# Window attention of the decode samples: from VectorE multiply-adds behind the state loop to matmuls ahead of it

## The chip, the cores and the metric

One Trainium2 chip, all 8 cores, each with an eighth of the work: 2048 tokens of a prompt and 16 of the 128 decode samples. The metric is the device time of the slowest core, in microseconds. Some executions fall in a slower state, in which the cores of one die or of both run at a lower granted clock; the comparisons below use fast runs alone.

A second measure is needed, because most of what is at stake lies in one short stretch. I call it the **sample stretch**: from the first matmul of the samples' input projection to the first activation of the last feed-forward's norm. It is read from the timeline of each of the eight cores of the profiled execution, and I quote the median of the eight, or the slowest core's value where I say so. In the kernel before it is 397.1 us in the median and 403.0 on the slowest core.

## The reference, cut to what matters

A layer is a half-step feed-forward, a mixer and a second half-step feed-forward. The mixer has four mLSTM heads and eight heads of window attention (SWA) with two shared key/value heads. For a decode sample the attention looks at 128 cached keys and values and at its own new one, with a sink:

```python
k_all = concatenate([buf_k, k]); v_all = concatenate([buf_v, v])
s = einsum('bqkgd,bskd->bkgqs', qg, k_all) * dh ** -0.5
mx = maximum(max(s), sink); p = exp(s - mx)
p = p / (sum(p) + exp(sink - mx))
o = einsum('bkgqs,bskd->bqkgd', p, v_all)
```

with 16 samples per core, 128 + 1 positions, two key/value heads of 64 and four query heads to each. The mLSTM of a sample updates a state of four 128x128 matrices (`c_new = decay * c + w * v k^T`) and reads it with q.

## The kernel before

Each core runs two passes over its tokens (feed-forward, then a pipelined mixer), then `sample_mixer` for its 16 samples, then the last feed-forward. A small scheduler derives the waits from keys: each operation names what it reads and writes, and a wait is made for the last writer, and before a write for the readers. Two names that share a key wait for one another, whether the bytes overlap or not. The parts of `sample_mixer` that matter:

```python
# mLSTM state loop: 4 groups of 4 samples
for bt in range(4):
    dma('sp', Cst, sC0_d[...], ['bigs'], ['bigs', 'Cst'], 'cst')        # 1 MB of state
    dma('sp', qrow, scr_d[0, ...].to_broadcast(...), ['scr0', 'bigs'], ['qrow'], 'qrow')  # 1 MB
    dma('sp', krow, scr_d[1, ...].to_broadcast(...), ['scr1', 'bigs'], ['krow'], 'krow')  # 1 MB
    prod = Cst * qrow; Cq = reduce(prod)                                # VectorE
    for j in range(16): Cst[j] *= decay[j]; Cst[j] += krow[j] * wv[j]   # VectorE
    dma('sp', sC_d[...], Cst, ['Cst'], [], 'cout')
# ... outputs of the mLSTM half into yTs[:, 0:4]; norms of q and k ...
# attention: one (sample, head) per partition, 128 of them
for g_, kv, p0, hd in PO:          # 8 x 4 small transfers: q, new k, new v, sink
    dma('sp', qx[p0:p0 + NS, :], qns[:, hd * 64:(hd + 1) * 64], ...)
    # [cut: kxn, vxn, sinkx alike]
load_kv(cK_d)                      # 8 transfers: each key head loaded for its 4 query heads
for d_ in range(64): Sx += Kx[:, :, d_] * qx[:, d_]        # VectorE, 128x128 each
load_kv(cV_d)                      # into the same buffer Kx
# [cut: softmax]
for d_ in range(64): ox[:, d_] = sum(Px * Kx[:, :, d_])    # VectorE
# [cut: 8 transfers back, cast, 4 transposes into yTs[:, 4:8]]
# output projection of the samples: 16 matmuls of yTs with w_out
```

`qrow` and `krow` name the key `bigs`, which the load of `Cst` writes, so they wait until it has landed.

Names used below: `rep` holds the gate factors of the 16 samples, sent through DRAM so that all 128 partitions get them; `wv` is v times one of these factors, the product that first needs `rep`; the first product of a group is `Cst * qrow`, 128x2048; `gon` is the gain of the mLSTM's output norm. In the changed kernel I call the part of the attention ahead of the state loop, from the norms to the scores, the **prelude**; `snew` is the score of a sample's own new key, `Vnd` its new value and `Vdup` the V cache, both written twice in bf16. SP is the queue from which nearly all these transfers are issued, in order.

## Time and profile before

| kernel before | |
|---|---|
| time, median of 4 runs | 3423.82 us (3419.25 to 3429.88) |
| sample stretch, slowest core | 403.0 us |
| of it the attention (norms to transposed result) | 218.8 us |
| VectorE's waits for the K and V caches in it | 76.5 + 56.9 us |
| three gaps between the groups of the state loop | 53.0 us of VectorE idle |
| last feed-forward, matmul part | 480 us at clock 0.99 |

Read it in this order: the slices show where TensorE is empty, the table of windows prices the hole, the timeline shows its order, the chain shows what waits for what. The lines stand in the prediction.

### The profile page before, as it was taken

How to read it: one execution, taken by the hardware profiler on the slowest of the kernel's cores; microseconds unless marked ns; L12 is line 12 of the kernel's file. 1: busy time of each engine (PE TensorE's matmuls, PEld its weight loads, DVE VectorE, ACT ScalarE, POOL GpSimd, SP SyncE). 2: the span in 40 equal slices, each digit the busy share in tenths (PEclk: the TensorE clock that was granted, in tenths of full speed). 3: DMA queues.
4: the chain of work that ended last, by engine and by line, in shares of the span. 5: the costliest groups of instructions: out<-in, count | busy, mean ns of one | idle time of the engine just before them, and what ended most of it. 6: DMA issues, size and time to landing. Idle time of an engine off the chain costs nothing.

```text
span 3423.5 us, 37344 instructions; the slowest of 8 cores (3394.0 to 3423.5 us)
## 1 busy us (share of the span) xinstructions
PE 2189.6 (64%) x12789; PEld 1145.4 (33%) x12789; DVE 1124.3 (33%) x2719; ACT 752.6 (22%) x1760; POOL 108.3 (3%) x151
## 2 busy tenths in 40 slices
PE   0499999565189999755655555555300001699999
PEld 0244444343144444333433333333100001344444
DVE  1223233454212222334434344343343222122223
ACT  1310100332420101133333433333100003311100
POOL 0000000000000100000000000000000000000000
PEclk9999999776599999977766777667655555799999
DMA  6032330503220402240000000000032892122222
GB/s 147 1 50 32 43 42 2 78 1 95 48 38 13 62 13 44 36 66 1 1 1 1 1 1 1 1 1 2 18 124 75 61 49 44 19 32 44 32 44 99
DMA packets 152241, 124.93 MB, mean 36 GB/s; under 512 B 42956, under 2 KB 132340, under 8 KB 151000
## 3 DMA queue, kind: packets, MB, share of 16 engines
q0 software_dynamic: 93744, 65.58, 14.0%
q1 hardware_dynamic: 58312, 56.98, 8.7%
q8 instruction: 105, 1.72, 0.2%
q14 instruction: 80, 0.66, 0.1%
HBM read 174.82 MB, written 15.24 MB: 56 GB/s over the span
## 4 chain that ended last, share of the span: by engine, by line
PE 56%; DVE 16%; ACT 9%; issue 8%; DMA 7%; SPq 4%; DVEq 1%; ACTq 0%; POOL 0%; POOLq 0%
PE ps L215 52%; SPq L212 4%; PE ps L218 3%; ACT sb_hT L228 3%; ACT sb_hn L228 2%; DVE sb_hn L257 2%; DMA sb_big<-win 2%; ACT sb_tmpC L228 2%; DMA sb_gain<-n 1%; DVE sb_CT L812 1%; DVE sb_hT L767 1%; ACT sb_sg L228 1%; DMA sb_big<-sC 1%; DVEq L124 1%; DVE sb_mixb L1105 1%
## 5 line engine op out<-in xcount | busy, mean ns | idle before, releaser
L215 PE MATMUL ps<-sb_hT,sb_wgu 128*128 128x512 bf16 (+1 forms) x4928 | 937.8, 351 | 1.2 <-ACT sb_hT L228 1.2
L215 PEld LDWEIGHTS ps<-sb_hT,sb_wgu 128*128 128x128 bf16 x4928 | 433.1, 98 | 506.5 <-issue 12.2
L215 PE MATMUL ps<-sb_big 128*128 128x512 bf16 (+1 forms) x2200 | 476.9, 379 | 0.0
L306 DVE TENSOR_TENSOR sb_big<-sb_sg,ps 128x512 bf16<-128x512 f32 x308 | 185.4, 613 | 756.7 <-PE ps L215 753.5
L228 ACT ACTIVATE sb_sg<-ps 128x512 f32<-128x512 f32 x308 | 165.8, 538 | 1101.8 <-PE ps L215 1101.7
L215 PEld LDWEIGHTS ps<-sb_big 128*128 128x128 bf16 (+1 forms) x2200 | 213.6, 97 | 259.9 <-issue 2.5
L322 DVE SCALAR_TENSOR_TENSOR sb_x<-ps,sb_x 128x512 f32<-128x512 f32 x288 | 199.2, 692 | 258.1 <-PE ps L215 258.1
L215 PE MATMUL ps<-sb_big,sb_hT 128*128 128x512 bf16 (+3 forms) x944 | 270.1, 448 | 8.5 <-DMA sb_big<-win 7.4
L218 PE MATMUL ps<-sb_identb,sb_hn 128*128 128x128 bf16 (+1 forms) x528 | 66.1, 303 | 298.6 <-DVE sb_hn L257 297.9
L228 ACT ACTIVATE sb_hT<-ps 128x1024 bf16<-128x1024 bf16 (+5 forms) x201 | 159.3, 792 | 397.3 <-PE ps L218 321.6
L218 PE MATMUL ps<-sb_identb,sb_hT 128*128 128x128 bf16 (+1 forms) x345 | 38.8, 261 | 323.3 <-DVE sb_hT L767 84.0
L218 PEld LDWEIGHTS ps<-sb_identb,sb_hn 128*128 128x128 bf16 (+1 forms) x528 | 51.5, 138 | 310.4 <-issue 310.4
L215 PEld LDWEIGHTS ps<-sb_big,sb_hT 128*128 128x128 bf16 (+1 forms) x944 | 104.0, 116 | 139.3 <-issue 94.1
L257 DVE SCALAR_TENSOR_TENSOR sb_hn<-sb_x,sb_stat,sb_gain 128x1024 bf16<-128x1024 f32 x48 | 61.7, 1285 | 249.8 <-ACT sb_stat L228 189.5
L218 PEld LDWEIGHTS ps<-sb_identb,sb_hT 128*128 128x128 bf16 (+1 forms) x345 | 26.5, 115 | 345.5 <-issue 345.5
L218 PE MATMUL ps<-sb_identb,sb_mixb 16*128 16x16 bf16 x4 | 0.3, 170 | 219.7 <-DVE sb_mixb L1127 219.7
L215 PE MATMUL ps<-sb_hT,sb_big 128*128 128x128 bf16 (+2 forms) x1600 | 115.3, 236 | 16.2 <-DMA sb_big<-win 16.2
L215 PEld LDWEIGHTS ps<-sb_hT,sb_big 128*128 128x128 bf16 (+1 forms) x1600 | 104.3, 102 | 28.7 <-issue 25.2
L212 POOL DMA_DIRECT2D sb_wgu<-wg x33 | 29.8, 903 | 2516.0 <-DVE sb_tmpA L1144 1648.4
L215 PE MATMUL ps<-sb_wgu,sb_hn 128*128 128x512 bf16 x256 | 92.5, 541 | 20.3 <-ACT sb_hn L228 20.3
L215 PE MATMUL ps<-sb_mixb,sb_onesf 128*128 128x64 f32 x2 | 0.7, 433 | 164.0 <-DVE sb_mixb L1066 164.0
L215 PE MATMUL ps<-sb_hT,sb_selT 4*128 4x1 f32 (+1 forms) x384 | 77.2, 305 | 0.0
(224 smaller groups left out, 1695.1 us busy)
## 6 DMA issues: line engine op xcount, KB each, us to landing
sb_wgu<-wg POOLq DMA_DIRECT2D x33, 512.0 KB, 7.8
sb_wgu<-wu POOLq DMA_DIRECT2D x33, 512.0 KB, 9.4
sb_big<-wd POOLq DMA_DIRECT2D x66, 256.0 KB, 9.8
sb_big<-win POOLq DMA_DIRECT2D x10, 1024.0 KB, 28.2
sb_x<-xa SPq DMA_DIRECT2D x16, 512.0 KB, 22.9
sb_x<-xb SPq DMA_DIRECT2D x16, 512.0 KB, 12.3
sb_big<-scr SPq DMA_DIRECT2D x8, 1024.0 KB, 6.9
yb<-sb_x SPq DMA_DIRECT2D x16, 512.0 KB, 2.6
```

Source lines behind the costliest of these rows:

```text
L124: eng.wait_ge(sems[key], v)
L212: P.add(q, lambda e: e.dma_start(out=out, in_=in_), r=r, w=w, dma=key)
L215: P.add('pe', lambda e: e.matmul(out, lhsT, rhs, start=start, stop=stop), r=r, w=w)
L218: P.add('pe', lambda e: e.transpose(out, in_, ident), r=r, w=w)
L228: P.add('act', lambda e: e.activation(out, in_, func, **kw), r=r, w=w)
L257: dve(lambda e: e.scalar_tensor_tensor(hs, xap, rs, gain[0:nt, :], ALU.mult, ALU.mult), [xkey, sk_, 'gain'], ['hn%d' % slot])
L306: dve(lambda e, ao=ao, sgs=sgs, ups=ups: e.tensor_tensor(ao, sgs, ups, ALU.mult), ['sg%d' % s2, 'b%d' % (2 + s2)], ['act%d.%d' % (jl, ti)])
L322: dve(lambda e, xh=xh, pb=pb: e.scalar_tensor_tensor(xh, pb, 0.5, xh, ALU.mult, ALU.add), ['b%d' % bk, xkey], [xkey])
L767: dve(lambda e, h=h, qo=qo: e.scalar_tensor_tensor(qnS[:, qo:qo + 64], qaps[:, h * 64:(h + 1) * 64], rq[:, h:h + 1], gqb, ALU.mult, ALU.mu ...
L812: dve(lambda e, h=h: e.scalar_tensor_tensor(CTv[:, h, :], CTv[:, h, :], decay_[:, h:h + 1], psb[4][:, h * 128:(h + 1) * 128], ALU.mult, AL ...
L1105: dve(lambda e, d_=d_: e.scalar_tensor_tensor(Sx, Kx[:, :, d_], qx[:, d_:d_ + 1], Sx, ALU.mult, ALU.add), ['Kx'] + M, M)
```

## The change

The intent: do the scores and the weighted sum on TensorE, load each cache once, start both loads early, and place the attention so that its latencies lie in other waits. The core of the diff (cuts marked):

```diff
-        dma('sp', n0s, sn0_d, [], WINKEYS + ACTKEYS + ['bigs'], 'sio')
+        dma('sp', n0s, sn0_d, [], WINKEYS + ACTKEYS + ['bigs', 'Cst', 'qrow', 'krow', 'prod'], 'sio')
+        dma('sp', K_all, cK_d.rearrange("b s f -> s b f"), [], HK + ['Kall'], 'kall')
+        dma('sp', V_all, cV_d.rearrange("b s f -> s b f"), [], HK + ['Vall'], 'vall')
 ...     # gates; rep goes through DRAM to be broadcast; wv = R(1) * vT
+        # norms of q and k (moved here), qpm = cast of q, 4 transposes -> qsT
+        # snew = q.k_new, by a product, a reduce and a small matmul
+        for quad in range(4):                      # 16 fp32 transposes of K, ScalarE evicts
+            ... tr(psb[bk][...], K_all[:, quad * 4 + j, :], identf) ...
+        Vdup = V_all twice, in bf16                # 2 VectorE copies of 128x2048
+        for kv in range(2):
+            for b in range(NS): mm(psb[4 + kv][:, b * 4:b * 4 + 4], KT[pr, b, :], qsT[pr, :, b], ...)
+        # STs, one transpose -> S_ps: one (sample, head) per partition again
         for bt in range(4):
-            dma('sp', Cst, ..., ['bigs'], ['bigs', 'Cst'], 'cst')
-            dma('sp', qrow, ..., ['scr0', 'bigs'], ['qrow'], 'qrow')
-            dma('sp', krow, ..., ['scr1', 'bigs'], ['krow'], 'krow')
+            dma('sp', Cst, ..., [], ['Cst'], 'cst')
+            dma('sp', qrow, ..., ['scr0'], ['qrow'], 'qrow')
+            dma('sp', krow, ..., ['scr1'], ['krow'], 'krow')
+            if bt == 0: # 16 sink transfers, 4 cache outputs
 ...         # the group's work and its store, unchanged
+            if bt == 0: # softmax on S_ps, transposes of P, 2 + 32 matmuls with Vnd and Vdup,
+                        # eviction straight into yTs[:, 4:8]
-        # the whole VectorE attention, its 40 small transfers and 16 cache loads
```

More of the change, by code (lines that the diff above doesn't have):

```diff
@@ L167, in build_nc @@
     swam_d = din("swam", [128, 256]); swam0_d = din("swam0", [128, 256]); amask_d = din("amask", [128, 2])
-    sel_d = din("sel", [4, 512])
+    sel_d = din("sel", [4, 512]); esel_d = din("esel", [128, 16])
     yb_d = dout("yb", [TOK, D]); ys_d = dout("ys", [NS, D])
@@ L192, in build_nc @@
     maskbig = sb("maskbig", [128, 128]); swam = sb("swam_t", [128, 256]); swam0 = sb("swam0_t", [128, 256])
-    amask = sb("amask_t", [128, 2]); selT = sb("selT", [68, 512])
+    amask = sb("amask_t", [128, 2]); selT = sb("selT", [4, 512]); esel = sb("esel_t", [128, 16])
     epsb = sb("epsb", [128, 1]); onesb = sb("onesb", [128, 128], BF16); onesf = sb("onesf", [128, 128])
@@ L242, in build_nc @@
     dma('sp', amask[:, :], amask_d, [], ['amask'], 'c0')
+    dma('sp', esel[:, :], esel_d, [], ['esel'], 'c0')
     dve(lambda e: e.memset(selT[:, :], 0.0), [], ['selT'])
@@ L997, in sample_mixer @@
         dma('sp', m0t, sm0_d, ['tmpA'], ['tmpA'], 'G_sin')
-        dma('sp', n0s, sn0_d, [], WINKEYS + ACTKEYS + ['bigs'], 'sio')
+        dma('sp', n0s, sn0_d, [], WINKEYS + ACTKEYS + ['bigs', 'Cst', 'qrow', 'krow', 'prod'], 'sio')
+        R_ = hT[:, :]
+        K_all = R_[:, 0:4096].bitcast(F32).rearrange("p (b f) -> p b f", f=128)
+        V_all = R_[:, 4096:8192].bitcast(F32).rearrange("p (b f) -> p b f", f=128)
+        dma('sp', K_all, cK_d.rearrange("b s f -> s b f"), [], HK + ['Kall'], 'kall')
+        dma('sp', V_all, cV_d.rearrange("b s f -> s b f"), [], HK + ['Vall'], 'vall')
         T = ['tmpA']
@@ L1043, in sample_mixer @@
         M = ['mixb']
+        W = ['SW']
         dve(lambda e: e.tensor_tensor(wv3, R(1), vT_bh, ALU.mult), M, M)
+        for nm_, src, n_, gk_, dst in (('q', qa_t, 8, gqb, qns), ('k', ka_t, 2, gkb, kns)):
+            w_ = n_ * 64
+            dve(lambda e, src=src, w_=w_: e.tensor_tensor(tq[:, 0:w_], src, src, ALU.mult), T + ['bigs'], ['bigs'])
+            dve(lambda e, n_=n_, w_=w_: e.tensor_reduce(sst[0:NS, 0:n_], tq[:, 0:w_].rearrange("p (h n) -> p h n", n=64), AX.X, ALU.add),
+                ['bigs'] + M, M)
+            act(sst[0:NS, 0:n_], sst[0:NS, 0:n_], AF.Ln, M + ['epsb'], M, bias=epsb[0:NS, :], scale=1.0 / 64)
+            act(sst[0:NS, 0:n_], sst[0:NS, 0:n_], AF.Exp, M, M, scale=-0.5)
+            for h in range(n_):
+                dve(lambda e, h=h, src=src, dst=dst, gk_=gk_: e.scalar_tensor_tensor(
+                    dst[:, h * 64:(h + 1) * 64], src[:, h * 64:(h + 1) * 64], sst[0:NS, h:h + 1], gk_[0:NS, :], ALU.mult, ALU.mult),
+                    T + M + ['gqb', 'gkb', 'bigs'], ['bigs'])
@@ new lines, in sample_mixer @@
+        KT = R_[:, 8192:10240].rearrange("p (b s) -> p b s", s=128)
+        Vdup = R_[:, 10240:14336].rearrange("p (b k r d) -> p b k r d", k=2, r=2, d=64)
+        PTb = R_[:, 14336:14464]; qsT = R_[:, 14464:14528].rearrange("p (g b) -> p g b", b=NS)
+        STs = R_[:, 14528:14784].bitcast(F32); Pnb = R_[:, 14784:14912]; psel = R_[:, 14912:14944].bitcast(F32)
+        qpm = bigf[0:NS, 10368:10624].bitcast(BF16)
+        tq2 = bigf[0:NS, 10624:11136]; snw = bigf[0:NS, 11136:11144]; Ls = bigf[0:NS, 11144:11272]
@@ new lines, in sample_mixer @@
+        Vnd = bigf[0:NS, 11272:11400].bitcast(BF16).rearrange("p (k r d) -> p k r d", k=2, r=2)
+        PnT = bigf[0:NS, 11400:11464].bitcast(BF16)
+        snew = sst[:, 8:9]; mxx = sst[:, 9:10]; nmx = sst[:, 10:11]; rs_ = sst[:, 11:12]; pn_ = sst[:, 12:13]; es_ = sst[:, 13:14]
+        dve(lambda e: e.tensor_copy(qpm.rearrange("p (g k d) -> p g k d", g=4, k=2), qns.rearrange("p (k g d) -> p g k d", k=2, g=4)),
+            ['bigs'], ['qpm'])
+        tq_ps = psb[3][:, :].bitcast(BF16)
+        for g_ in range(4):
+            tr(tq_ps[:, g_ * NS:(g_ + 1) * NS], qpm[:, g_ * 128:(g_ + 1) * 128], identb[0:NS, 0:NS], ['qpm', 'identb'], ['b3'])
@@ new lines, in sample_mixer @@
+        act(qsT, tq_ps[:, 0:64].rearrange("p (g b) -> p g b", b=NS), AF.Copy, ['b3'] + HK, ['qsT'])
+        dve(lambda e: e.tensor_tensor(tq2.rearrange("p (k g d) -> p k g d", k=2, g=4), qns.rearrange("p (k g d) -> p k g d", k=2, g=4),
+                                      kns.rearrange("p (k d) -> p k d", d=64).unsqueeze(2).to_broadcast([NS, 2, 4, 64]), ALU.mult),
+            ['bigs'], ['tq2'])
+        dve(lambda e: e.tensor_reduce(snw, tq2.rearrange("p (h d) -> p h d", d=64), AX.X, ALU.add), ['tq2'], ['snw'])
@@ new lines, in sample_mixer @@
+        dve(lambda e: e.tensor_tensor(Ls.rearrange("p (b h) -> p b h", h=8), snw.unsqueeze(1).to_broadcast([NS, NS, 8]),
+                                      identf[0:NS, 0:NS].unsqueeze(2).to_broadcast([NS, NS, 8]), ALU.mult), ['snw', 'identf'], ['Ls'])
+        mm(psb[3][:, 256:257], Ls, onesf[0:NS, 0:1], True, True, ['Ls', 'onesf'], ['b3'])
+        dve(lambda e: e.tensor_copy(snew, psb[3][:, 256:257]), ['b3'], W)
+        for r_ in range(2):
+            dve(lambda e, r_=r_: e.tensor_copy(Vnd[:, :, r_, :], va_t.rearrange("p (k d) -> p k d", d=64)), T, ['Vnd'])
@@ new lines, in sample_mixer @@
+        for quad in range(4):
+            bk = 1 + quad % 2
+            for j in range(4):
+                tr(psb[bk][:, j * 128:(j + 1) * 128], K_all[:, quad * 4 + j, :], identf[:, :], ['Kall', 'identf'], ['b%d' % bk])
+            act(KT[:, quad * 4:(quad + 1) * 4, :], psb[bk][:, :].rearrange("p (j s) -> p j s", s=128), AF.Copy, ['b%d' % bk] + HK, ['KT'])
+        for r_ in range(2):
+            dve(lambda e, r_=r_: e.tensor_copy(Vdup[:, :, :, r_, :], V_all.rearrange("p b (k d) -> p b k d", d=64)), ['Vall'] + HK, ['Vdup'])
@@ new lines, in sample_mixer @@
+        for kv in range(2):
+            pr = slice(kv * 64, (kv + 1) * 64)
+            for b in range(NS):
+                mm(psb[4 + kv][:, b * 4:b * 4 + 4], KT[pr, b, :], qsT[pr, :, b], True, True, ['KT', 'qsT'], ['b%d' % (4 + kv)])
+        STs4 = STs.rearrange("p (b k g) -> p b k g", k=2, g=4)
+        for kv in range(2):
+            dve(lambda e, kv=kv: e.tensor_copy(STs4[:, :, kv, :], psb[4 + kv][:, 0:64].rearrange("p (b g) -> p b g", g=4)),
+                ['b%d' % (4 + kv)] + HK, ['STs'])
@@ L1045, in sample_mixer @@
+        S_ps = psb[6][:, 0:128]
+        tr(S_ps, STs, identf[:, :], ['STs', 'identf'], ['b6'])
         for bt in range(4):
             b0_ = bt * 4
-            dma('sp', Cst, sC0_d[b0_:b0_ + 4].rearrange("b h v k -> v (b h) k"), ['bigs'], ['bigs', 'Cst'], 'cst')
+            dma('sp', Cst, sC0_d[b0_:b0_ + 4].rearrange("b h v k -> v (b h) k"), [], ['Cst'], 'cst')
             dma('sp', qrow, scr_d[0, b0_:b0_ + 4, :].rearrange("(o b) f -> o b f", o=1).to_broadcast([128, 4, 512]).rearrange("p b (h k) -> p (b h) k", k=128) if False else
@@ L1049, in sample_mixer @@
                 scr_d[0, b0_:b0_ + 4, :].rearrange("(o b) (h k) -> o (b h) k", o=1, k=128).to_broadcast([128, 16, 128]),
-                ['scr0', 'bigs'], ['qrow'], 'qrow')
+                ['scr0'], ['qrow'], 'qrow')
             dma('sp', krow, scr_d[1, b0_:b0_ + 4, :].rearrange("(o b) (h k) -> o (b h) k", o=1, k=128).to_broadcast([128, 16, 128]),
-                ['scr1', 'bigs'], ['krow'], 'krow')
+                ['scr1'], ['krow'], 'krow')
+            if bt == 0:
+                for b in range(NS):
+                    dma('sp', sinkx[b * 8:(b + 1) * 8, :], snk_d.rearrange("o h -> h o"), [], W, 'G_snk')
@@ L1053, in sample_mixer @@
+            if bt == 0:
+                dma('sp', sk_d[:, 0:127, :], cK_d[:, 1:128, :], [], [], 'sout')
+                dma('sp', sv_d[:, 0:127, :], cV_d[:, 1:128, :], [], [], 'sout')
+                dma('sp', sk_d[:, 127, :], kns, ['bigs'], [], 'sout')
+                dma('sp', sv_d[:, 127, :], va_t, T, [], 'sout')
             dve(lambda e: e.tensor_tensor(prod, Cst, qrow, ALU.mult), ['Cst', 'qrow'], ['prod'])
@@ L1061, in sample_mixer @@
             dma('sp', sC_d[b0_:b0_ + 4].rearrange("b h v k -> v (b h) k"), Cst, ['Cst'], [], 'cout')
+            if bt == 0:
+                dve(lambda e: e.tensor_reduce(mxx, S_ps, AX.X, ALU.max), ['b6'] + W, W)
+                dve(lambda e: e.tensor_tensor(mxx, mxx, snew, ALU.max), W, W)
+                dve(lambda e: e.tensor_scalar(mxx, mxx, 0.125, None, ALU.mult), W, W)
+                dve(lambda e: e.tensor_tensor(mxx, mxx, sinkx, ALU.max), W, W)
+                dve(lambda e: e.tensor_scalar(nmx, mxx, -1.0, None, ALU.mult), W, W)
+                act(Px, S_ps, AF.Exp, ['b6'] + W, W, bias=nmx, scale=0.125, accum=rs_)
+                act(pn_, snew, AF.Exp, W, W, bias=nmx, scale=0.125)
+                act(es_, sinkx, AF.Exp, W, W, bias=nmx)
+                dve(lambda e: e.tensor_tensor(rs_, rs_, pn_, ALU.add), W, W)
+                dve(lambda e: e.tensor_tensor(rs_, rs_, es_, ALU.add), W, W)
+                dve(lambda e: e.reciprocal(rs_, rs_), W, W)
+                dve(lambda e: e.tensor_scalar(Pnb, Px, rs_, None, ALU.mult), W + HK, ['Pnb'])
+                dve(lambda e: e.tensor_tensor(pn_, pn_, rs_, ALU.mult), W, W)
+                dve(lambda e: e.tensor_scalar(psel, esel[:, :], pn_, None, ALU.mult), W + ['esel'] + HK, ['psel'])
+                tp_ps = psb[6][:, 128:192].bitcast(BF16)
+                tr(tp_ps, Pnb, identb[:, :], ['Pnb', 'identb'], ['b6'])
+                act(PTb, tp_ps, AF.Copy, ['b6'] + HK, ['PTb'])
+                tr(psb[7][0:NS, 0:128], psel, identf[:, :], ['psel', 'identf'], ['b7'])
+                dve(lambda e: e.tensor_copy(PnT, psb[7][0:NS, 0:128]), ['b7'], ['PnT'])
+                OT_ps = psb[4][:, 256:384]
+                OT4 = OT_ps.rearrange("p (b k g) -> p b k g", k=2, g=4)
+                PnT4 = PnT.rearrange("p (b k g) -> p b k g", k=2, g=4)
+                for kv in range(2):
+                    P.add('pe', lambda e, kv=kv: e.matmul(OT4[:, :, kv, :], Vnd[:, kv, :, :].rearrange("p r d -> p (r d)"), PnT4[:, :, kv, :],
+                                                          start=kv == 0, stop=False, skip_group_check=True), r=['Vnd', 'PnT'], w=['b4'])
+                for b in range(NS):
+                    for kv in range(2):
+                        c4 = b * 8 + kv * 4
+                        P.add('pe', lambda e, b=b, kv=kv, c4=c4: e.matmul(OT_ps[:, c4:c4 + 4], Vdup[:, b, kv, :, :].rearrange("p r d -> p (r d)"), PTb[:, c4:c4 + 4],
+                                                                          start=False, stop=True, skip_group_check=True), r=['Vdup', 'PTb'], w=['b4'])
+                OTv = OT_ps.rearrange("p (b j r) -> p r j b", j=4, r=2)
+                for r_ in range(2):
+                    pr = slice(r_ * 64, (r_ + 1) * 64)
+                    act(yTs[pr, 4:8, :], OTv[pr, r_, :, :], AF.Copy, ['b4'], ['yTs'])
@@ L1076, in sample_mixer @@
             dve(lambda e, h=h: e.tensor_scalar(yTs[:, h, :], num3[:, :, h], gonT[:, h:h + 1], None, ALU.mult), M + ['CTb'], ['yTs'])
-        for nm_, src, n_, gk_, dst in (('q', qa_t, 8, gqb, qns), ('k', ka_t, 2, gkb, kns)):
-            w_ = n_ * 64
-            dve(lambda e, src=src, w_=w_: e.tensor_tensor(tq[:, 0:w_], src, src, ALU.mult), T + ['bigs'], ['bigs'])
-            dve(lambda e, n_=n_, w_=w_: e.tensor_reduce(sst[0:NS, 0:n_], tq[:, 0:w_].rearrange("p (h n) -> p h n", n=64), AX.X, ALU.add),
-                ['bigs'] + M, M)
-            act(sst[0:NS, 0:n_], sst[0:NS, 0:n_], AF.Ln, M + ['epsb'], M, bias=epsb[0:NS, :], scale=1.0 / 64)
-            act(sst[0:NS, 0:n_], sst[0:NS, 0:n_], AF.Exp, M, M, scale=-0.5)
-            for h in range(n_):
-                dve(lambda e, h=h, src=src, dst=dst, gk_=gk_: e.scalar_tensor_tensor(
-                    dst[:, h * 64:(h + 1) * 64], src[:, h * 64:(h + 1) * 64], sst[0:NS, h:h + 1], gk_[0:NS, :], ALU.mult, ALU.mult),
-                    T + M + ['gqb', 'gkb', 'bigs'], ['bigs'])
@@ L1088, in sample_mixer @@
-        PO = [(g_, kv, g_ * 32 + kv * 16, kv * 4 + g_) for g_ in range(4) for kv in range(2)]
-        for g_, kv, p0, hd in PO:
-            dma('sp', qx[p0:p0 + NS, :], qns[:, hd * 64:(hd + 1) * 64], ['bigs'] + M, M, 'G_qx')
-            dma('sp', kxn[p0:p0 + NS, :], kns[:, kv * 64:(kv + 1) * 64], ['bigs'] + M, M, 'G_qx')
-            dma('sp', vxn[p0:p0 + NS, :], va_t[:, kv * 64:(kv + 1) * 64], T + M, M, 'G_qx')
-            dma('sp', sinkx[p0:p0 + NS, :], snk_d[0:1, hd:hd + 1].to_broadcast([NS, 1]), M, M, 'G_qx')
@@ L1094, in sample_mixer @@
-        dma('sp', sk_d[:, 0:127, :], cK_d[:, 1:128, :], [], [], 'sout')
-        dma('sp', sv_d[:, 0:127, :], cV_d[:, 1:128, :], [], [], 'sout')
-        dma('sp', sk_d[:, 127, :], kns, ['bigs'], [], 'sout')
-        dma('sp', sv_d[:, 127, :], va_t, T, [], 'sout')
-        def load_kv(src_d, key):
-            for g_, kv, p0, hd in PO:
-                dma('sp', Kx[p0:p0 + NS, :, :], src_d[:, :, kv * 64:(kv + 1) * 64], [], HK + ['Kx'], key)
-        load_kv(cK_d, 'G_kxk')
-        dve(lambda e: e.tensor_scalar(Sx, Kx[:, :, 0], qx[:, 0:1], None, ALU.mult), ['Kx'] + M, M)
@@ L1104, in sample_mixer @@
-        for d_ in range(1, 64):
-            dve(lambda e, d_=d_: e.scalar_tensor_tensor(Sx, Kx[:, :, d_], qx[:, d_:d_ + 1], Sx, ALU.mult, ALU.add), ['Kx'] + M, M)
-        load_kv(cV_d, 'G_kxv')
-        snew = sst[:, 8:9]; mxx = sst[:, 9:10]; nmx = sst[:, 10:11]; rs_ = sst[:, 11:12]; pn_ = sst[:, 12:13]; es_ = sst[:, 13:14]
-        dve(lambda e: e.scalar_tensor_tensor(junk[:, 0:64], qx, 0.125, kxn, ALU.mult, ALU.mult, accum_out=snew), M, M)
-        dve(lambda e: e.tensor_reduce(mxx, Sx, AX.X, ALU.max), M, M)
@@ L1110, in sample_mixer @@
-        dve(lambda e: e.tensor_scalar(mxx, mxx, 0.125, None, ALU.mult), M, M)
-        dve(lambda e: e.tensor_tensor(mxx, mxx, snew, ALU.max), M, M)
-        dve(lambda e: e.tensor_tensor(mxx, mxx, sinkx, ALU.max), M, M)
-        dve(lambda e: e.tensor_scalar(nmx, mxx, -1.0, None, ALU.mult), M, M)
-        act(Px, Sx, AF.Exp, M, M, bias=nmx, scale=0.125, accum=rs_)
-        act(pn_, snew, AF.Exp, M, M, bias=nmx)
-        act(es_, sinkx, AF.Exp, M, M, bias=nmx)
-        dve(lambda e: e.tensor_tensor(rs_, rs_, pn_, ALU.add), M, M)
@@ L1118, in sample_mixer @@
-        dve(lambda e: e.tensor_tensor(rs_, rs_, es_, ALU.add), M, M)
-        dve(lambda e: e.reciprocal(rs_, rs_), M, M)
-        for d_ in range(64):
-            dve(lambda e, d_=d_: e.scalar_tensor_tensor(junk, Px, 1.0, Kx[:, :, d_], ALU.mult, ALU.mult, accum_out=ox[:, d_:d_ + 1]),
-                ['Kx'] + M, M)
-        dve(lambda e: e.scalar_tensor_tensor(ox, vxn, pn_, ox, ALU.mult, ALU.add), M, M)
-        dve(lambda e: e.tensor_scalar(ox, ox, rs_, None, ALU.mult), M, M)
-        for g_, kv, p0, hd in PO:
-            dma('sp', tq[:, hd * 64:(hd + 1) * 64], ox[p0:p0 + NS, :], M + ['bigs'], ['bigs'], 'G_ox')
@@ L1127, in sample_mixer @@
-        dve(lambda e: e.tensor_copy(ystok, tq), ['bigs'] + M, M)
-        tps = psb[3][:, :].bitcast(BF16)
-        for fc in range(4):
-            tr(tps[:, fc * NS:(fc + 1) * NS], ystok[:, fc * 128:(fc + 1) * 128], identb[0:NS, 0:NS], M + ['identb'], ['b3'])
-        act(yTs[:, 4:8, :], tps[:, 0:64].rearrange("p (c b) -> p c b", b=NS), AF.Copy, ['b3'], ['yTs'])
         for half in range(2):
@@ L1139, in sample_mixer @@
             dve(lambda e, xh=xh, pb=pb: e.tensor_tensor(xh, xh, pb, ALU.add), ['b%d' % (6 + half), 'xs'], ['xs'])
-        dve(lambda e: e.memset(rowst[0:NS, 0:1], 0.0), [], ['bigs', 'Cst', 'qrow', 'krow', 'prod', 'Kx', 'mixb', 'yTs'] + ACTKEYS + HK + ['tmpA'])
+        dve(lambda e: e.memset(rowst[0:NS, 0:1], 0.0), [], ['bigs', 'Cst', 'qrow', 'krow', 'prod', 'Kx', 'mixb', 'yTs', 'SW', 'Kall', 'Vall', 'KT', 'Vdup', 'PTb', 'qsT', 'STs', 'Pnb', 'psel', 'qpm', 'tq2', 'snw', 'Ls', 'Vnd', 'PnT'] + ACTKEYS + HK + ['tmpA'])
     def mixer_done():
@@ L1212, in make_in_maps @@
         wout=f(inp['w_out'])[0], n2=f(inp['ffn2_norm']), wg2=f(inp['ffn2_w_gate'])[0], wu2=f(inp['ffn2_w_up'])[0],
-        wd2=f(inp['ffn2_w_down'])[0], ident=ident, maskbig=maskbig, swam=swam, sel=sel)
+        wd2=f(inp['ffn2_w_down'])[0], ident=ident, maskbig=maskbig, swam=swam, sel=sel,
+        esel=np.repeat(np.eye(16, dtype=np.float32), 8, axis=0))
     maps = []
```

## The prediction

> **What bounds the kernel now.** I read the kernel for what each core does, then the page's 40 slices to find holes, then the table of windows to price the hole, then the timeline and the chain inside it. Every core runs two passes over its tokens (feed-forward, then mixer), then sample_mixer for its 16 decode samples, then the last feed-forward. The slices of the profile of before:
>
> ```profile
> PE   0499999565189999755655555555300001699999
> PEclk9999999776599999977766777667655555799999
> ```
>
> TensorE is the bound in the feed-forward blocks (nines), but slices 29 to 33, some 2445 to 2945 us, are nearly empty and at half clock. The busy time by stretch on the slowest core; columns are the stretch, its length, busy us and instructions of PE, PEld, DVE, ACT, POOL, clock, DMA share, GB/s:
>
> ```profile
> 2445.70:2623.40 177.70, 8.99 (x107) 5.48 (x107) 72.74 (x187) 2.33 (x10) 0.00 (x0) 0.53 0.31 98
> 2623.40:2842.20 218.80, 0.25 (x4) 0.19 (x4) 59.18 (x220) 2.31 (x9) 0.00 (x0) 0.50 0.71 49
> 2842.20:2848.60 6.40, 5.14 (x16) 1.72 (x16) 1.44 (x5) 0.00 (x0) 0.00 (x0) 0.75 0.00 0
> ```
>
> The first stretch is the sample mLSTM, the second the sample window attention (SWA), the third the sample output projection. No other work runs beside them; the feed-forward that follows needs the samples' x and the buffers, so the stretch is all on the path that sets the end. What the 218.8 us consist of, from the timeline (start, length, engine, line):
>
> ```profile
> 2623.43 0.67 DVE L1079 TENSOR_TENSOR sb_big<-sb_tmpA 16x512 f32<-16x512 f32 x1
> ...
> 2652.96 43.28 SPq L212 DMA_DIRECT2D sb_hT<-cK  x8
> 2707.64 0.36 DVE L1103 TENSOR_SCALAR sb_mixb<-sb_hT,sb_mixb 128x128 f32<-128x128 f32 x1 [76.50 <-DMA sb_hT<-cK]
> 2708.10 29.73 DVE L1105 SCALAR_TENSOR_TENSOR sb_mixb<-sb_hT,sb_mixb 128x128 f32<-128x128 f32 x56
> ...
> 2742.37 45.44 SPq L212 DMA_DIRECT2D sb_hT<-cV  x8
> ...
> 2802.74 0.38 DVE L1121 SCALAR_TENSOR_TENSOR sb_mixb<-sb_mixb,sb_hT 128x128 f32<-128x128 f32 x1 [56.87 <-DMA sb_hT<-cV]
> ...
> 2834.87 4.86 SPq L212 DMA_DIRECT2D sb_big<-sb_mixb  x8
> ```
>
> The reader sees a strict series: norms of q and k (2623.4 to 2631.1), 32 small rearranging transfers that SP issues one by one and then the cache of K in eight transfers (VectorE waits 76.5 us), 64 multiply-adds for the scores (34 us), then only the cache of V into the same buffer (56.9 us of waiting), 64 multiply-accumulates (31 us), eight transfers back, a transpose, and the projection at 2842.34. Nothing overlaps.
>
> The last view is the chain of waits between two groups of the mLSTM state loop before it:
>
> ```profile
> 2508.03 5.09 DMA sC<-sb_big
> 2513.25 6.31 DMA sb_big<-sC
> 2519.63 6.00 DMA sb_big<-scr
> 2525.72 2.30 DVE sb_big L1053
> ```
>
> Store of the state, load of the next, then the broadcast rows, one after the other: 17.7 us in which VectorE stands still (17.7, 17.1 and 18.1 in the three gaps).
>
> **What the Trainium skill says.** "DMA: Bandwidth & Descriptors", section "Anatomy of one DMA", gives a fixed 2 us and a part that grows with the bytes. The trace agrees on the fixed part (tiny transfers land after 1.7 us) but a 1 MB state load takes 6.3 us, not the 4.4 of its fit; I use 6.3. The same page, "Why small descriptors are slow", says 256 B pieces carry overhead. In this trace the K cache in 256 B pieces, copied four times (8 x 512 KB = 4.2 MB), takes 54.7 us, 77 GB/s; the state in 512 B pieces runs at 166 GB/s. "VectorE: DVE Perf Modes", section "Mode 2x_2P", lets a copy from SBUF move two elements a cycle, also in fp32, not from PSUM. The trace agrees: a 128x128 cast takes 227 ns from SBUF and 284 from PSUM, a 16x512 cast 416 ns against some 675 for PSUM copies. "TensorE: Matmul & The Clock Gate", Part 1, says an idle array falls to half clock and warms within some 3.4 us of work. It agrees: 0.50 in the hole, 0.75 in the projection.
>
> **The change, part by part.**
>
> Removed: everything from 2623.43 to the eviction of the transposed attention result at 2842.2, 218.8 us. After the change the projection needs only the mLSTM half of yTs, which VectorE finishes at 2623.5 in the trace; so the projection moves up by 2842.34 - 2623.6 = 218.7 us, before anything is added.
>
> Added before the state loop. VectorE's wv product waits for the broadcast of rep and ends at 2481.2. Then, in program order: norms of q and k as before (2631.1 - 2623.4 = 7.7 us, only moved); qpm cast 0.5 (16x512, 416 ns + gap); tq2 0.8 and its reduce 0.8 (16x512, 680 ns each); Ls 0.4; the small matmul and the copy of snew, 0.7; two Vnd copies 0.6. That is 11.5, at 2492.7. Two Vdup copies of 128x2048: twice 2048/1.92 + 150 = 1.2 us if the double rate holds, else 2.3 (the 2048-element product takes 2.29). Beside these TensorE transposes 16 K tiles: four fp32 transposes took 0.60 us warm, so 0.6 to 1.2 each quad at half clock, with ScalarE evictions (0.6) behind; then 32 score matmuls with four columns (64 matmuls 128x16 took 1.77 us), about 1 to 2 us; two STs copies 0.5. TensorE starts at about 2491.8 and VectorE gets to the first product at about 2499.5 (estimate). The data for it are there by then: Cst and both rows no longer wait for one another, and the K and V caches (1 MB each, 512 B pieces, issued near 2456) land by about 2468, while VectorE works on gates. In before that product began at 2489.66. So the first group starts some 10 us later: **+10**.
>
> Added inside the loop, after group 0: softmax, 13 VectorE instructions at 0.16 to 0.3, three ScalarE exponentials at 0.3 to 0.6, two transposes, 34 small matmuls, two evictions. As VectorE order counts, about 6 to 7 us until PnT is copied; the gap it stands in is over 15 us. Hidden: **0**. The 16 sinkx transfers cost SP 16 x 0.61 = 9.8 us of issue, the four cache outputs 2.4; starting after snew at 2492 they end near 2505, before the first state store at about 2518. Hidden: **0**.
>
> Changed in the gaps: qrow and krow lose their wait for Cst. Store 5.1 stays. Cst alone moves for 6.3 - 2 = 4.3 us, the rows for 5.4 to 6.3 less 2, about 3.8; together on the same 16 engines about 8.1 + 2 = 10.1 instead of 12.3 us. The DMA share was 0.59 in the one stretch and 0.60 to 0.86 in the other, so there is little room to do better. Three gaps by 2.1: **-6**.
>
> At the start, one more constant to load: 0.5 us of issue, **+0.5**.
>
> Sum: -218.7 + 10 - 6 + 0.5 = -214. From 3423.8 this gives **3209 us**, 6.3% less.
>
> **The rivals.** (1) The wait only moves: the caches' loads delay the small transfers of the gates and the state loads. For: all are on SP's queue in order. Against: K and V without the fourfold copies are 2 MB instead of 8.4, and near 2456 to 2470 the queue carries almost nothing. If V lands at 2485 and holds up Cst and rep, I lose 10 to 15 us: 3220 to 3225. (2) Concurrency in the gaps is worth more: if the rows hide wholly under Cst, a gap falls to 5.1 + 6.5 = 11.6, and 12 us more are won: 3197. If it is worth nothing: 3215. (3) The prelude is dearer: cold fp32 transposes, Vdup at single rate, waits between four engines. At double my 10 us: 3219. (4) The final feed-forward gets slower for want of rest, by a lower granted clock. Against: the feed-forward of 1020 to 1400 us follows busy mixer work at once and shows 1.00 in each 100 us, like the last one. A clock of 0.9 there would cost 50 us: 3260; I give it 3%. (5) The hole is not on the path: nothing runs beside it, TensorE is busy 0.25 us in 218.8; I give this nothing.
>
> **Range and chances.** Rivals 1 to 3 each move the result by some 6 to 12 us and are independent; the runs of before spread by 5 us. So 3197 to 3222 for 8 in 10. Two per cent is 68 us; no rival takes back two thirds of 214. Faster 0.98, same 0.015, slower 0.005.
>
> **What would show it.** Right: the cK and cV waits of 76.5 and 56.9 us are gone; the stretch between the pass-two mixer and the last feed-forward falls from 403 to about 189 us; the first 128x2048 product starts about 18 us after the wv product; the gaps between groups are about 15.5 us with the softmax inside; the projection starts at once after the four 128x16 scalings; the last feed-forward still takes 480 us at clock 1.00. Wrong: wv ends well after 2481 (rival 1), gaps of 12 or 17 us (rival 2), VectorE or TensorE over 25 us between wv and the product (rival 3), a clock under 1.00 after the hole (rival 4).

## The result, and the profile after

The changed kernel took 3211.09 us in the median of its first 11 runs (of the fast ones 3205 to 3214), the kernel before 3437.91 in 16 runs, of which seven are well above the others. The ratio of the fast runs is 0.9364, 95% interval 0.9347 to 0.938. (A ratio is the mean time of one kernel's fast runs over that of the other's of the same rounds, so not quite the ratio of the medians quoted.) The result was correct. The prediction said 3209 and 3197 to 3222.

The slices of the changed kernel, from its page; before, five slices (of 86 us) read 0 or 1; now three (of 80 us) do, and one reads 2. The slices at half clock go from five to three:

```profile
PE   0399999766329999986455555555552011999999
PEclk9999999877659999997676776766766555999999
```

The table of windows of its slowest core, same columns as in the prediction. The rows are the projections and the state loop with the attention inside, the end of the mLSTM, the output projection, and the matmul part of the last feed-forward:

```profile
2444.20:2620.50 176.30, 15.95 (x195) 10.74 (x195) 82.14 (x211) 7.13 (x24) 0.00 (x0) 0.53 0.37 116
2620.50:2627.90 7.40, 0.90 (x3) 0.68 (x3) 2.75 (x12) 0.57 (x2) 0.00 (x0) 0.50 0.50 142
2627.90:2635.00 7.10, 5.80 (x16) 1.85 (x16) 1.48 (x5) 0.00 (x0) 0.00 (x0) 0.68 0.00 0
...
2728.00:3209.00 481.00, 478.05 (x2516) 219.93 (x2516) 132.96 (x212) 58.17 (x112) 25.89 (x36) 0.99 0.27 48
```

and the last of these before the change, which the prediction does not show:

```profile
2943.00:3423.00 480.00, 477.19 (x2508) 219.51 (x2508) 132.92 (x212) 57.88 (x111) 25.89 (x36) 0.99 0.25 48
```

The row of 218.8 us is gone, and 176.3 + 7.4 = 183.7 us stand where 177.7 stood: the attention adds 6 us net, some 12 ahead of the loop less some 6 won in the gaps. VectorE's busy time in that part rises from 72.7 to 84.9 us (82.14 + 2.75), while 59.2 us of the old attention vanish. The last feed-forward takes what it took. The timeline ahead of the first group, with the rows that set its pace:

```profile
2453.87 0.84 SPq L212 DMA_DIRECT2D sb_hT<-cK  x1
...
2462.11 0.70 SPq L212 DMA_DIRECT2D sb_hT<-cV  x1
...
2471.28 0.38 SPq L212 DMA_DIRECT2D sb_mixb<-scr  x1
2471.83 2.95 SPq L212 DMA_DIRECT2D sb_big<-sC  x1
2474.88 9.26 SPq L212 DMA_DIRECT2D sb_big<-scr  x2
2483.51 0.27 DVE L1051 TENSOR_TENSOR sb_mixb<-sb_mixb 128x64 f32<-128x64 f32 x1 [13.70 <-DMA sb_mixb<-scr]
...
2492.11 0.22 ACT L228 ACTIVATE sb_hT<-ps 128x64 bf16<-128x64 bf16 x1 [1.82 <-PE ps L218]
...
2493.95 3.95 PE L218 MATMUL ps<-sb_identf,sb_hT 128*128 128x128 f32 x16
...
2494.65 2.54 DVE L1094 CAST sb_hT<-sb_hT 128x2048 bf16<-128x2048 f32 x2
...
2499.46 0.23 DVE L1101 COPY sb_hT<-ps 128x64 f32<-128x64 f32 x1 [2.28 <-PE ps L215]
...
2500.06 2.29 DVE L1121 TENSOR_TENSOR sb_big<-sb_big 128x2048 f32<-128x2048 f32 x1
```

L1051 is the wv product, L1121 the first product of the state loop, 16.55 us later. There is no idle time before L1121: its data were there, VectorE's own series and the transposes on TensorE set the start. Two things the reader can see that the prediction did not have: V's load is issued 8.2 us after K's, and VectorE waits 13.70 us for the rep broadcast, not 10.1.

The chain between two groups, the counterpart of the chain in the prediction:

```profile
2518.49 5.14 DMA sC<-sb_big
2523.75 0.77 SPq L212
2524.61 8.71 DMA sb_big<-scr
2533.49 2.30 DVE sb_big L1121
```

Store, then state and rows together: the first row, the one that the product needs, lands 9.6 us after the state's issue at 2523.75, where 12.3 stood before. The softmax lies in this gap; behind it VectorE still waits 9.8 of the 15.1 us.

### The profile page after: what moved, and what is told of

The parts are those of the page before. It is cut to its first block, busy times and chain, and to the rows that moved or that the text cites. A ratio compares the mean times of both kernels' runs of the same rounds, so it can differ in the third digit from the quotient of the medians.

```text
span 3209.8 us, 37207 instructions; the slowest of 8 cores (3181.7 to 3209.8 us)
## 1 busy us (share of the span) xinstructions
PE 2199.9 (69%) x12876; PEld 1152.0 (36%) x12876; DVE 1077.8 (34%) x2537; ACT 755.7 (24%) x1767; POOL 108.3 (3%) x151
## 4 chain that ended last, share of the span: by engine, by line
PE 60%; DVE 15%; ACT 10%; issue 8%; DMA 5%; SPq 1%; DVEq 1%; ACTq 0%; POOL 0%; POOLq 0%
PE ps L215 56%; PE ps L218 4%; ACT sb_hT L228 3%; ACT sb_hn L228 2%; DVE sb_hn L258 2%; DMA sb_big<-win 2%; ACT sb_tmpC L228 2%; DMA sb_gain<-n 1%; DVE sb_CT L813 1%; DVE sb_hT L768 1%; SPq L212 1%; ACT sb_sg L228 1%; DMA sb_big<-scr 1%; ACT sb_scal L228 1%; DVEq L124 1%
## 5 line engine op out<-in xcount | busy, mean ns | idle before, releaser
L228 ACT ACTIVATE sb_hT<-ps 128x1024 bf16<-128x1024 bf16 (+6 forms) x207 | 162.1, 783 | 402.0 <-PE ps L218 326.4
L215 PE MATMUL ps<-sb_smallb,sb_hT 128*128 128x64 bf16 (+3 forms) x328 | 28.5, 215 | 68.5 <-DVE sb_scal L817 60.9
L228 ACT ACTIVATE sb_tmpC<-sb_tmpA,sb_scal 128x256 bf16<-128x256 f32 x128 | 64.5, 504 | 20.8 <-DVE sb_scal L858 11.3
## 6 DMA issues: line engine op xcount, KB each, us to landing
sb_x<-xb SPq DMA_DIRECT2D x16, 512.0 KB, 12.3
```

Source lines behind the costliest of these rows:

```text
L215: P.add('pe', lambda e: e.matmul(out, lhsT, rhs, start=start, stop=stop), r=r, w=w)
L228: P.add('act', lambda e: e.activation(out, in_, func, **kw), r=r, w=w)
```

## The experiments

Twelve runs, all correct. Medians over the eight cores of each profiled execution; "first product" is the time from the start of the sample stretch to the first product of the state loop, "wv" that to the wv product where it comes first. Times are medians of the fast runs, with their number. The ratio is given where enough fast runs of the kernel before stood beside it: the chip of the first four runs gave only two, and e7 and e8 stand on one fast execution each.

| run | wv | first product | sample stretch | time, fast runs | ratio to before |
|---|---|---|---|---|---|
| kernel before | 34.4 | 42.3 | 397.1 | see above | 1 |
| changed kernel | 36.1 | 52.7 | 185.6 | see above | 0.9364 |
| e1 relaxed waits only | 33.9 | 39.7 | 390.8 | 3420.1 (3) | - |
| e2 waits back | 35.3 | 51.8 | 192.7 | 3218.9 (4) | - |
| e3 old place | 35.4 | 41.3 | 199.2 | 3227.5 (4) | - |
| e4 old place, late caches | 34.1 | 40.0 | 198.3 | 3229.3 (4) | - |
| e5 rep first | 33.2 | 49.7 | 184.8 | 3213.3 (4) | 0.9369 |
| e6 prelude early | - | 43.5 | 176.8 | 3205.7 (4) | 0.9350 |
| e7 extra work before | 35.8 | 58.8 | 190.7 | 3219.7 (1) | - |
| e8 extra work in gap | 35.9 | 52.4 | 184.2 | 3208.4 (1) | - |
| e9 K early, old form | 59.4 | 78.6 | 373.2 | 3403.3 (3) | 0.9916 |
| e10 two buffers | 35.6 | 52.2 | 152.8 | 3178.7 (2) | 0.9266 |
| e11 both | - | 41.7 | 143.1 | 3169.2 (4) | 0.9239 |
| e12 changed kernel again | 36.4 | 53.0 | 185.6 | 3211.8 (4) | 0.9365 |

### e1, e2: the relaxed waits alone, and undone

In the kernel before, only the keys of the loads are changed as in the diff above (e1). In the changed kernel, only this is put back (e2):

```diff
-                ['scr0'], ['qrow'], 'qrow')
+                ['scr0', 'Cst'], ['qrow'], 'qrow')
-                ['scr1'], ['krow'], 'krow')
+                ['scr1', 'Cst'], ['krow'], 'krow')
```

> The kernel before with only the relaxed waits: the state and its two rows no longer wait for one another. The sample stretch (first sample projection matmul to the first activation of the last feed-forward) was 403.0 us before. My theory: the three gaps fall from about 17.7 to 15.3 us and the first group starts some 2 us sooner, so 394 to 396 us, ratio to before about 0.9975. Rival: the gaps are bound by what the 16 engines move, so nothing falls: 402 to 404 us, ratio 1.000.

> The changed kernel with only those waits put back (rows wait for the landed state). The stretch of the changed kernel is 190.9 us. If the rows and the state together are what makes the rep broadcast land 3.6 us later than before, gaps cost about 7 us more and the prelude starts about 3.6 us sooner: 194 us. Rival: the loads of the K and V caches delay rep; then rep stays late and the stretch is 198 us.

e1: the stretch falls by 6.3 us in the median. The distance from the first to the fourth product, three groups' work and three gaps, falls from 107.0 to 99.1, by 8, so the gaps do share the engines better, and the first product comes 2.6 us sooner. The absolute expectation of 394 to 396 was meant for the slowest core and cannot be tested: one die of this execution ran at 0.79 against 0.80 of the other, and its core 1 shows 403.1. The die that was not disturbed has 382 to 396, in the median 388.5, where the same four cores of the kernel before have 396.5. The time has no ratio, because only two fast runs of the kernel before stood beside it; the claim rests on the stretch. e2 agrees from the other side: the same distance is 107.2 against 99.1 and the stretch grows by 7.1. But the wv product moved by only 0.8 us towards where it was. My expectation said rep would come back by 3.6 us and soften the loss to 3; it did not, and the loss is the rival's 7.

### e3, e4: the attention in its old place, then with late loads too

The new form is kept, the code between the wv product and the loop, the softmax block and the sink transfers are put behind the loop's outputs (e3); in e4 the two cache loads stand there too.

```diff
-        # prelude here, softmax block inside `if bt == 0`
         for bt in range(4): ...
         # ... mLSTM half of yTs ...
+        # (e4: K_all and V_all loads here)
+        # prelude; sink transfers; softmax block
         # output projection
```

> The changed kernel with the attention in its old place, after the state loop; caches still loaded early, matmul form kept. My theory: the form carries the gain, the place little. The first state product starts about 12 us sooner, 16.5 us of prelude and 7 of softmax stand behind the loop, and the 16 sink transfers (about 10 us) come onto the path for some 5: stretch about 206 us, +15. Rival: the place (hiding) carries the gain: over 250 us.

> As the run with the attention in its old place, but with the caches of K and V loaded only there, as before the change. My theory: 2 MB in two loads of 6 to 8 us lie mostly beside the norms and the sink transfers: +2 to +6 us over that run, about 208 to 212 us. Rival: late loading is what cost the 133 us of cache waits, whatever the form: over 280 us.

e3 is 13.6 us longer than the changed kernel, as expected (15). In the median e4 is not longer than e3 (198.3 against 199.2), but two of its cores, the slowest among them, have 204 and 207 us, where e3's longest has 201.6. The timeline of the slowest core shows the copy of the transposed q (the same as at 2492.11 in the changed kernel), the sink transfers and the softmax's first operation:

```profile
2627.63 0.22 ACT L228 ACTIVATE sb_hT<-ps 128x64 bf16<-128x64 bf16 x1 [4.91 <-DMA sb_hT<-cV]
...
2628.90 9.06 SPq L212 DMA_DIRECT2D sb_mixb<-snk  x16
...
2640.04 0.29 DVE L1143 TENSOR_REDUCE sb_mixb<-ps 128x1 f32<-128x128 f32 x1 [5.49 <-DMA sb_mixb<-snk]
```

The caches land for the most part while VectorE does the norms. The copy waits for V all the same, since both write the keys of the shared buffer: it starts some 3 us after the transposes' end here, 2 on core 0 and some 5 on core 5. In the median this is made up by a first product 1.3 us sooner than in e3. What the softmax waits for in both runs are sixteen transfers of 32 bytes that SP issues one after the other. So from 397.1 to 198.3 us, 199 of the 211.5 us, comes without any hoisting: the form (one load of 1 MB per cache in place of 4.2 MB in eight pieces, no 40 rearranging transfers, matmuls for the 128 VectorE passes) and the relaxed waits, which e1 prices at 6 to 8. The place is worth the remaining 13. The parts of the form were not tried one by one; the trace before gives 133.4 us of the 218.8 as VectorE's waits for the caches and 59.2 as its work. e4's median falls below my 208 to 212; I had let the loads cost 2 to 6, and they do so on some cores only.

### e5: rep ahead of the state

```diff
-            ['scr2', 'mixb'], ['mixb'], 'sio')
+            ['scr2', 'mixb'], ['mixb', 'repk'], 'sio')
-            dma('sp', Cst, ..., [], ['Cst'], 'cst')
+            dma('sp', Cst, ..., ['repk'], ['Cst'], 'cst')
```

> The changed kernel with the first state load (and the rows behind it in the queue) held until the rep broadcast has landed. In the changed kernel rep takes 12.1 us to land, before 8.5. My theory: it shares the 16 engines with 3 MB of state and rows; alone it lands in 4 to 6 us, the prelude starts that much sooner and the state still lands before the first product: stretch about 184 to 186 us against 190.9. Rival: its 64-byte pieces cost what they cost: rep still takes over 8 us and the stretch stays at 189 to 193 us.

The wv product and the first product come 3 us sooner in the median, so sharing with the state does delay rep, but two cores still show wv at 38, and the slowest core's rep took 11.7 us from issue to landing. Against the expected 5 to 7 us the stretch gains 0.8 and the time nothing (0.9369 and 0.9364); the first-to-fourth distance is 101 in place of 99 and eats most of the 3. Why the gaps are longer there I did not find out. Both theories fail in part.

### e6: the prelude ahead of the wv product

The prelude's scratch columns get the key `SW` in place of `mixb`, which rep writes; then the block moves above the wv product.

```diff
-        dve(lambda e: e.tensor_tensor(wv3, R(1), vT_bh, ALU.mult), M, M)
         # norms (M -> W) ... scores, S_ps
+        dve(lambda e: e.tensor_tensor(wv3, R(1), vT_bh, ALU.mult), M, M)
```

> The changed kernel with the attention's prelude (norms to scores) ahead of the wv product, so that VectorE does it while it would wait 13.7 us for rep. My theory: the +12 us of the prelude are then hidden and the first product waits for the rows, at about 16 us before the wv product's old successor, that is about 12 us sooner: stretch about 179 us. Rival: the prelude is bound by the chain over TensorE and ScalarE and by the landing of V, and cannot start sooner: 188 us or more.

The stretch falls by 8.8 us and the first product comes 9 us sooner; expected were 12. Four cores, the slowest with its 5.3 us among them, then wait 2.5 us or more for the rows ahead of the first product; the other four wait less than 1 us and are bound by VectorE's series. The time is 3205.7 (0.9350, interval 0.9334 to 0.9366, which overlaps that of the changed kernel: the gain is shown by the stretch and not by the time). The prelude's cost in the sum was thus a matter of order, and most of it can be hidden.

### e7, e8: the same needless work in two places

Eight repetitions of a 16x512 product (678 ns each in the trace, 6.2 us with their gaps), ahead of the loop (e7) or behind the softmax in the first gap (e8).

> The changed kernel with eight needless 16x512 products (0.78 us each, 6.2 us) on VectorE just ahead of the state loop. My theory: the prelude is on the path there: +6 us, stretch 197 us. Rival: the first product waits for its data anyway: +0 to +2 us.

> The same eight products in the gap after group 0, behind the softmax. My theory: the gap has 9.8 us left, so they are hidden: +0 us, 191 us. Rival: VectorE work is in series wherever it stands: +6 us, 197 us.

Ahead of the loop the first product moves by 6.1 us (52.7 to 58.8) and the stretch by 5.1. In the gap the stretch does not grow (184.2), and VectorE's idle time there falls from 9 to 10 us to about 3. So work in the gap is free up to the room that is left there, as the prediction's zero for the softmax says, and work ahead of the loop is paid in full, as its plus for the prelude says.

### e9: the old form with K loaded early

In the kernel before, the eight K loads are issued on ScalarE's queue ahead of the state loop.

```diff
+        load_kv(cK_d, 'G_kxk', 'act')
         for bt in range(4): ...
-        load_kv(cK_d, 'G_kxk')
```

> The kernel before (attention on VectorE, old place) with only the fourfold load of the K cache issued ahead of the state loop, on ScalarE's queue. My theory: the 76.5 us wait falls to some 24 (the small rearranging transfers stay) and the state loop loses about 10 us to sharing the engines: stretch about 360 us against 403.0, ratio about 0.988. Rival: the 256-byte pieces keep the 16 engines full, the state loads only queue behind them: stretch 385 us or more.

The stretch falls by 24 us (on the slowest core to 384.8), the time to 0.9916 (0.9894 to 0.9938): nearer to the rival. VectorE's waits in the slowest core:

```profile
DVE sb_big L1058 <- DMA sb_big<-scr: 70.5, 4, 20.6
DVE sb_mixb L1121 <- DMA sb_hT<-cV: 56.6, 1, 56.6
DVE sb_mixb L1044 <- DMA sb_mixb<-scr: 28.6, 1, 28.6
DVE sb_mixb L1103 <- DMA sb_mixb<-snk: 21.0, 1, 21.0
DVE sb_hn L257 <- ACT sb_stat L228: 16.9, 4, 4.5
DVE sb_tmpA L1031 <- DMA sm<-sb_tmpA: 11.6, 1, 11.6
```

The wait of 76.5 us for K is gone and what is left before the scores is the 21.0 us for the small transfers. But everything small that shares the engines pays: VectorE waits 28.6 us for rep where it waited 10.1, and 11.6 for a store of 256 bytes where it waited 2.0. The wv product comes at 59 us in place of 34. A transfer in 256-byte pieces is hidden from its own reader and not from its neighbours. The same early load in the new form, a quarter of the bytes in pieces of 512 and on SP's queue, did no such harm; which of the three differences spares the neighbours was not tried.

### e10, e11, e12: two buffers, both, and a control

`Cst` and `krow` alternate between their old space and that of K_all and V_all once these are used up; the next group's loads are issued after this group's first product. The two large cache outputs move behind the last store.

```diff
+        Cst_s = [Cst, R_[:, 0:4096]...]; krow_s = [krow, R_[:, 4096:8192]...]
+        loads(0)
         for bt in range(4):
             # prod, Cq
+            if bt < 3: loads(bt + 1)
             # the 32 updates; store
+            if bt == 3: # sk and sv cache outputs
```

> The changed kernel with two buffers for the state and for one of the rows (in the space of K and V once they are used up), so that the loads of the next group run under VectorE's work on this one. My theory: of 46.5 us of gaps about 37 go, the softmax then stands on the path: stretch about 154 us, time about 3172. Rival: 3 MB in and 1 MB out per group take about as long as VectorE's 18.4 us, the loads stay the bound and under 20 us are won: 171 us or more.

> Two buffers and the early prelude together. My theory: the two gains add up, -12 and -37: stretch about 142 us, time about 3161. Rival: the first loads then come in the way of the prelude, or the gains overlap: 150 us or more.

> The changed kernel unaltered, as control on the chip of these runs: 3205 to 3214 us, stretch 189 to 192 us, ratio to before 0.936.

e10 is as expected (152.8 in the median, 153.8 on the slowest core; 154): the products start 23.5, 18.6 and 18.2 us apart and VectorE idles before none, so the loads fit under 18.4 us of work, and the softmax costs its 5.1 us openly. With the early prelude (e11) the time is 3169.2 us, 0.9239: 1.3% below the changed kernel (3169.2 over 3211.8), the fastest version. The two gains add up: 8.8 (e6) and 32.8 (e10) make 41.6, and the stretch falls by 42.5, from 185.6 to 143.1 in the median (139.8 to 146.5 over the cores), near the expected 142. The chain of the slowest core of e10 shows what both runs still lose:

```profile
2582.23 0.67 PE ps L215 x2
2584.41 8.14 DMA sb_mixb<-gon
2594.70 5.32 PE ps L215 x16
```

A transfer of 2 KB (gon) took 1.3 us in the changed kernel, where only the last state store was ahead of it, and takes 8.1 here, where I had put 2 MB of cache output ahead of it in SP's queue. TensorE waits 9 to 11 us for it on six cores of e11 and 13 to 13.7 on the two with the longest stretches. Issued behind gon instead, these outputs should give back some 6 us (an estimate: TensorE waited about 9.1 us for gon on most cores of e10 and 3.0 in the changed kernel); it was not run. The control repeated the changed kernel: 3211.8 us, 0.9365, stretch 185.6.

## Why the prediction was right

Its steps, on the two profiled slowest cores (core 1 of before, core 7 of after), counted from the start of the sample stretch:

| term of the sum | predicted | measured |
|---|---|---|
| first product later by | +10 | +12.0 (43.9 to 55.9); medians +10.4 |
| three gaps | -6 | -6.2 (first to fourth product 108.0 to 101.8); medians -8 |
| softmax, sink transfers | 0 | 0 (e8; no wait for them in the changed kernel) |
| from the fourth product to the end of the stretch | -218.7 | -217.9 (251.1 to 33.2) |
| start of the kernel | +0.5 | not seen: the stretch began 1.5 us sooner on that core; medians 2439.0 and 2439.2 |
| whole time, profiled slowest cores | -214 | -213.7 (3423.5 to 3209.8) |

The stretch gives -212.1, the time before it -1.5, and the last feed-forward takes 574.7 and 574.8 us, norm included. That the whole fits to 0.3 us is luck: the first product came 2.0 us later than predicted, and the early start that makes up for it is a difference between two cores, whose starts lie 23 and 26 us apart over the cores of the two executions. The mechanism is confirmed by the terms, each within 2.0 us, and not by the last digit.

The removal was the safe part: with TensorE busy 0.25 of 218.8 us, nothing of it was hidden work. What could have gone wrong was the replacement, and there three details were off, which cancelled in part.

First, the prediction let the wv product stay where it was. It came 4.1 us later on the core shown (35.3 to 39.4), 1.7 in the medians. Rival 1, that the wait only moves, holds to that extent. The early cache loads have a part in it: with late loads (e4) wv is at 34.1, with early ones in the same order (e3) at 35.4. The rows now issued together with the state may have another (e2, 0.8 us), and holding the state back gains 3 (e5). These are differences of the size of the scatter between cores, so how the 1.7 us divide stays open.

Second, from the end of wv to the first product it took 16.3 us, not the 18.3 worked out; the two Vdup copies run at the double rate (2.54 us together, where one product of 2048 elements takes 2.29) and TensorE's sixteen transposes took 3.95 us, within the 2.4 to 4.8 that four quads were given. TensorE and not VectorE is what ends it: VectorE stands 2.28 us before the scores are copied.

Third, K and V were said to load together. V's load waits for K to land, since both write all the keys of the shared buffer: SP waited 7.3 us. It did no harm here: V landed 6.2 us after its issue at 2462.11, so near 2468, as predicted, and the copy at 2492.11 waits for TensorE alone. In e4 the same shared keys do cost time.

The gaps came out as estimated from the shares of the engines: 15.1, 16.35 and 15.1 us on the slowest core, 15.5 expected. Rival 2's cheap gap of 11.6 did not appear: state and first row took 9.3 to 10.6 us together, and only the second buffer takes them off the path (e10). The output projection took 5.80 us, 0.7 more than before, at a mean clock of 0.68 in its window against 0.75, which no term had.

Rival 4, a slower last feed-forward, is out: 481 us at 0.99 after the shorter rest, 480 at 0.99 before.

One reading of the prediction is loose: slices 29 to 33 are 2482 to 2910 us of the span, not 2445 to 2945. Nothing was computed from it.

What the prediction left open is which part of the change earns the gain. By e3 and e4 it is the form, together with the relaxed waits (6 to 8 us); hoisting, the most intricate part of the diff, brings 13 us, 6% of the gain.

## What to carry to other kernels

Price a hole by its own window: if no engine works beside it and the next stage needs its result, nearly all of it is gain, and the uncertainty is only in what replaces it. Change the form first (here bytes loaded once, longer pieces, no rearranging transfers, and matmuls in place of vector passes, whose shares were not separated); hiding what is left was worth much less here, and only where the trace shows idle time that nobody else needs. Early loads are free for their reader but not for the small transfers that share their engines and queue: look at those before issuing megabytes ahead of them.

## What the Trainium skill lacked or had wrong

- "DMA: Bandwidth & Descriptors", section "Anatomy of one DMA": its fit of 2 us and bytes over 436 GB/s is stated for another issuing path and gives 4.4 us for a 1 MB load; the state load in 512 B pieces on SP's queue took 6.3 us. (A table of measured loads further down that page, for the other path too, has 6.15 us for 1 MB, so there the fit and not the load is off.) For the state and both rows queued together (3.1 MB) the fit gives 9.2 us as an estimate; in the three gaps the second row landed 11.8 to 13.5 us after the state's issue, the first row 9.3 to 10.6 us after it.
- The same page, section "Why small descriptors are slow": its example puts the overhead of a 256 B piece at 27%. Here 256 B pieces into 16 partitions ran at 77 GB/s and 512 B pieces into 128 at 166; piece and partitions were not separated.
- The same page: its sections read give no number for what a small transfer pays behind large ones. Here a 128 KB broadcast in 64 B pieces took 8.5 us with 1 MB behind it and 15.9 under the 4.2 MB of early K; a 2 KB load took 1.3 us behind the end of a 1 MB store and 8.1 behind 2 MB.
